# Attention of a hybrid backbone: weights times [values | ones] in full-width products, a PSUM bank per head

## The chip, the cores and the metric

One Trainium2 chip, one of its cores. The metric is the device time of one execution in microseconds, as the median of several runs of the same program.

## The reference

Two layers of a latent-token backbone work on 1024 latent and 256 context tokens of 1024 features. Each layer normalizes and modulates its input, projects it once, and splits the result into three mixers: grouped-query attention (8 heads of 64, 2 heads of keys and values), a long convolution (Hyena), and gated linear attention. Their outputs are normalized per head, put side by side, projected, and added to the stream; a SwiGLU block follows. The part that matters here:

```python
def gqa_attend(q, k, v):
    b, lq = q.shape[:2]
    qg = q.reshape(b, lq, ATTN_KV_HEADS, ATTN_GROUP, HEAD_DIM)
    s = jnp.einsum('bqkgd,bskd->bkgqs', qg, k, preferred_element_type=jnp.float32)
    p = jax.nn.softmax(s, axis=-1).astype(v.dtype)
    o = jnp.einsum('bkgqs,bskd->bqkgd', p, v)
    return o.reshape(b, lq, ATTN_WIDTH)

def head_rms_norm(x, g):
    shp = x.shape
    xh = x.reshape(shp[:-1] + (shp[-1] // HEAD_DIM, HEAD_DIM))
    return rms_norm(xh, g.reshape(-1, HEAD_DIM)).reshape(shp)
```

Latent queries read all 1280 keys, context queries (first layer alone) the 256 context keys. Everything is float32. Since the heads' outputs are RMS-normalized right after, the softmax need not be divided by its sum: with o the undivided output and S the sum of the weights, normalizing o/S with a constant eps is the same as normalizing o with eps times S squared.

## The kernel before, in words

The program is recorded through a tile framework whose scheduler sets the order on each engine; nothing in this part is ordered by hand. `phase1` makes the projections, `phase2` the three mixers, `phase34` the output projection and the SwiGLU. Matmuls of projections, scores and transforms use operands split into a high and a low part (fp32r); a product of two float32 tiles is two passes on TensorE and leaves two records.

In `phase2` the long convolution (`hyena`) is recorded first, then the linear attention (`gla`), then the attention, which the scheduler fills in wherever an engine is free. The eight PSUM banks are dealt to roles (L1380): banks 0 to 2 for the score maxima, 3 and 4 for the scores, bank 5 for the outputs, 6 and 7 for the other two mixers.

The attention runs in jobs: a key-value head, a pair of its query heads, a block of queries (512, 512, and 256 context queries). That is 12 jobs in the first layer and 8 in the second, 20 in all.

- `attn_q` (L1011) prepares a head's queries and finds the row maximum of the scores: for each 128 queries and each block of keys a product into a bank of role 0 and a maximum on VectorE (L1031, L1032), then a transpose brings the maxima to one row of the second operand, Q2. The queries of job i + 1 are recorded ahead of the products of job i.
- `attn_o` (L1040) goes over the key chunks of 128. For each of the two heads: two score products (K1 with Q1, K2 with Q2), then the exponential on ScalarE into a tile p, from a ring of 6 (L1056). Then the product of p with the 64 columns of values: head 0's goes to partitions 0 to 63 of the one output bank, head 1's to partitions 64 to 127, each by one half of the array's columns (L1060). GpSimd adds up the p tiles of each head (L1068).
- `attention` (L1071) then sums the accumulated weights over the partitions by a product with 64 columns of ones per head (L1095), copies the output, squares both, takes the mean square per head by a product with `blk` (L1102), adds eps times the squared sums on VectorE (L1103), and calls `headnorm`, which takes the reciprocal root (`rsqrt`, L189: Ln, Exp and Square on ScalarE, two steps on VectorE) and writes to DRAM.

All three of the outputs, the sums and the mean squares use bank 5 in turn.

```python
            for j in range(2):
                self.mm(X[64 * j:64 * j + 64], V[:, kc], ps[j], kc == k0, kc == 9)
```

## Time and profile before

| | |
|---|---|
| three runs, us | 3710.39 (median), 3722.3, 3709.04 |
| the profiled execution, span | 3712.2 us, 1.8 us above that median; no time of its own outside the span is given |
| PE busy | 3563.2 us, 96% |
| VectorE (DVE) busy | 2014.1 us, 54% |
| GpSimd (POOL) busy | 1353.5 us, 36% |
| ScalarE (ACT) busy | 1088.0 us, 29% |
| mean granted clock of TensorE | 0.978 |

One execution is shown by a hardware profiler. An engine's busy time is the union of its instructions' records. A matmul's record runs on past the point at which the next one starts, so for a stream of matmuls the distance from start to start is its price, and the record's length is not. "PEld" is the load of the stationary operand. L numbers are lines of the kernel.

### The profile page before, as it was taken

The numbers are of one execution on the slowest core, as the hardware profiler recorded it, in microseconds if no ns is written. First come the engines' busy times: TensorE is split into PE (matmuls) and PEld (weight loads), VectorE is DVE, ScalarE is ACT, GpSimd is POOL, SyncE is SP. The second block draws the span as 40 slices with busy tenths as digits, with TensorE's granted clock in tenths as the row PEclk, the third lists the DMA queues.
The fourth block names the chain that finished last, engine by engine and source line by source line (L and its number), as shares of the span: only waits on it lengthen the run. The fifth ranks groups of instructions, "written<-read, shape, count | busy, mean of one in ns | idle before, by whom it ended". The sixth has DMA issues, their size and how long they took to land.

```text
span 3712.2 us, 46254 instructions
## 1 busy us (share of the span) xinstructions
PE 3563.2 (96%) x17903; PEld 2693.5 (73%) x17903; DVE 2014.1 (54%) x3271; ACT 1088.0 (29%) x1956; POOL 1353.5 (36%) x960
## 2 busy tenths in 40 slices
PE   8999899999999999999999899899999999999999
PEld 4789845445677888888888688865445788888887
DVE  6755667863677665644223773757753533223233
ACT  4243233553422111111111333333554421111112
POOL 2424564664333111111111541656764542221221
PEclk9999999999999999999999899999999999999999
DMA  9333311120633323321111333411112421111111
GB/s 329 99 124 123 120 33 43 56 81 20 212 110 99 95 80 89 90 66 54 49 35 46 107 111 116 150 49 42 35 70 71 139 63 51 40 57 46 52 40 57
DMA packets 275804, 310.63 MB, mean 84 GB/s; under 512 B 18680, under 2 KB 205727, under 8 KB 274304
## 3 DMA queue, kind: packets, MB, share of 16 engines
q1 hardware_dynamic: 269279, 287.75, 24.6%
q0 software_dynamic: 2560, 13.89, 1.0%
q10 hardware_dynamic: 3744, 6.03, 0.4%
q8 instruction: 140, 2.29, 0.3%
q14 instruction: 81, 0.66, 0.1%
HBM read 245.75 MB, written 61.87 MB: 83 GB/s over the span
## 4 chain that ended last, share of the span: by engine, by line
PE 75%; DVE 11%; POOL 4%; issue 3%; DMA 3%; ACT 1%; SPq 0%; DVEq 0%; POOLq 0%; ACTq 0%
PE ps L175 74%; PE ps L184 1%; POOL hss L928 1%; DMA nsq<-in_ada_w 1%; POOL hl L187 1%; DVE acc L329 1%; DVE mx L1032 1%; DVE sg L1138 1%; DMA yr<-y_d 0%; DVE h L1537 0%; POOL hy L936 0%; DVE sg L1150 0%; DVE sg L1151 0%; DVE nacc L365 0%; DVE hx L930 0%
## 5 line engine op out<-in xcount | busy, mean ns | idle before, releaser
L175 PE MATMUL ps<-u,hl 128*128 128x512 f32 (+1 forms) x6504 | 1384.4, 372 | 20.6 <-DVE u L403 6.2
L175 PEld LDWEIGHTS ps<-u,hl 128*128 128x128 f32 x6504 | 1136.3, 190 | 252.5 <-issue 14.9
L187 POOL TENSOR_TENSOR hl<-raw,hl 128x1024 fp32r<-128x1024 f32 x148 | 366.5, 2479 | 944.3 <-ACT hl L421 924.5
L175 PE MATMUL ps<-g,w 128*128 128x512 f32 (+1 forms) x2688 | 556.6, 367 | 10.0 <-DVE h L1537 3.4
L175 PEld LDWEIGHTS ps<-g,w 128*128 128x128 f32 x2688 | 466.6, 190 | 95.5 <-DVE h L1537 5.4
L1068 POOL TENSOR_TENSOR ac<-ac,p 128x512 f32<-128x512 f32 x256 | 354.7, 1394 | 159.4 <-ACT p L1057 158.8
L1498 DVE TENSOR_TENSOR s<-ps,s 128x512 f32<-128x512 f32 (+1 forms) x110 | 70.0, 637 | 614.7 <-PE ps L175 597.3
L1537 DVE SCALAR_TENSOR_TENSOR h<-ps,mod,h 128x512 f32<-128x512 f32 (+1 forms) x448 | 303.5, 687 | 181.8 <-PE ps L175 181.6
L175 PE MATMUL ps<-p,V 128*64 128x512 f32 x672 | 309.8, 607 | 4.7 <-ACT p L1057 2.5
L187 POOL TENSOR_TENSOR w<-raw,w 128x1024 fp32r<-128x1024 f32 x44 | 109.0, 2477 | 500.0 <-ACT w L421 499.9
L1032 DVE TENSOR_REDUCE mx<-ps 128x1 f32<-128x512 f32 (+1 forms) x400 | 221.0, 587 | 120.8 <-PE ps L175 119.8
L1057 ACT ACTIVATE p<-ps 128x512 f32<-128x512 f32 (+1 forms) x336 | 194.6, 586 | 286.8 <-PE ps L175 277.7
L175 PEld LDWEIGHTS ps<-Q,K 65*128 65x128 f32 (+1 forms) x672 | 105.0, 191 | 222.2 <-issue 209.8
L421 ACT CAST hl<-raw 128x1024 fp32r<-128x1024 f32 x148 | 154.9, 1049 | 303.9 <-PE ps L175 151.5
L329 DVE SCALAR_TENSOR_TENSOR acc<-nsq,silc,acc 128x512 f32<-128x512 f32 x252 | 210.6, 876 | 61.3 <-DMA nsq<-in_ada_w 60.6
L175 PE MATMUL ps<-Q,K 65*128 65x512 f32 (+1 forms) x672 | 242.2, 442 | 1.2 <-ACT p L1057 1.1
L175 PE MATMUL ps<-y,hl 128*128 128x512 f32 (+1 forms) x960 | 213.8, 381 | 13.2 <-DVE y L187 6.1
L175 PEld LDWEIGHTS ps<-y,hl 128*128 128x128 f32 x960 | 170.8, 194 | 59.3 <-DVE y L187 8.2
L421 ACT CAST w<-raw 128x1024 fp32r<-128x1024 f32 x44 | 46.2, 1051 | 491.8 <-PE ps L175 443.2
L175 PE MATMUL ps<-my,dft 128*128 128x256 f32 (+1 forms) x1176 | 166.8, 294 | 10.3 <-DVE my L187 9.7
L1499 ACT CAST g<-s 128x512 fp32r<-128x512 f32 (+1 forms) x110 | 63.3, 576 | 385.2 <-DVE s L1498 385.2
L175 PEld LDWEIGHTS ps<-my,dft 128*128 128x128 f32 x1176 | 159.1, 203 | 20.6 <-DVE my L187 13.7
(265 smaller groups left out, 4129.2 us busy)
## 6 DMA issues: line engine op xcount, KB each, us to landing
raw<-in_ffn_w SPq DMA_DIRECT2D x132, 512.0 KB
nsq<-in_ada_w SPq DMA_DIRECT2D x144, 256.0 KB
raw<-in_w_in SPq DMA_DIRECT2D x36, 512.0 KB
raw<-in_w_out SPq DMA_DIRECT2D x32, 512.0 KB
ada<-in_ada_w SPq DMA_DIRECT2D x24, 512.0 KB
h_d<-h SPq DMA_DIRECT2D x32, 256.0 KB
dft<-in_c_dft POOLq DMA_DIRECT2D x8, 1024.0 KB, 7.2
qd<-qT_d SPq DMA_DIRECT2D x64, 128.0 KB
```

The source lines that it names most:

```text
L175: self.nc.tensor.matmul(out, w, x, start=start, stop=stop)
L184: self.nc.tensor.transpose(out, in_, self.ident[:n, :n])
L187: eng.tensor_tensor(out=out, in0=x, in1=hi.bitcast(F32), op=ALU.subtract)
L329: nc.vector.scalar_tensor_tensor(out=acc[w], in0=raw, scalar=s, in1=acc[w], op0=ALU.mult, op1=ALU.add)
L421: self.nc.scalar.copy(hi, raw)
L928: nc.gpsimd.tensor_tensor(out=ss, in0=ss, in1=self.mh[:, :nh], op=ALU.pow)
L1032: nc.vector.tensor_reduce(out=mx[:, j, i:i + 1], in_=pm, op=ALU.max, axis=AX.X)
L1057: nc.scalar.activation(p, st, AF.Exp)
L1068: nc.gpsimd.tensor_tensor(out=acc[j], in0=x, in1=ps[j], op=ALU.add)
L1498: nc.vector.tensor_tensor(out=s, in0=p3, in1=s, op=ALU.mult)
L1499: nc.scalar.copy(gs[m][:, 0, o:o + n], s)
L1537: nc.vector.scalar_tensor_tensor(out=h, in0=ps, scalar=self.mod[l][:, 40 + k, w:w + 1], in1=h, op0=ALU.mult, op1=ALU.add)
```

## The change

- The values are stored per key-value head as 192 columns, values, ones, values: `V[:, kvh]`. A memset writes the ones, four loads the values.
- Head 0 takes columns 0 to 127 (values, ones), head 1 columns 64 to 191 (ones, values). A product now fills all 128 columns and one PSUM bank per head: 64 partitions get the outputs, the other 64 get the sum of the weights, once on each partition.
- The additions on GpSimd and the products with ones go.
- ScalarE copies the output halves of both banks into one tile, and squares the sum halves into another, whose halves then lie on the other head's partitions. The mean square and eps times the squared sums come together in one PSUM tile from two products, with `blk` and with `swap` (`blk` with its columns reversed). That tile comes from role 0, the banks of the maxima, and `rsqrt` reads it there.
- Banks: 0 and 1 for the maxima and these mean squares, 2 and 3 for the scores, 4 and 5 for the outputs. The ring of p has 4 tiles.

```diff
+    swap = np.ascontiguousarray(blk[:, ::-1])
...
-                self.V = self.t(ap, [P, 10, P], F32, "V", 1)
-                nc.sync.dma_start(out=self.V, in_=self.v_d)
+                self.V = self.t(ap, [P, 2, 10, 192], F32, "V", 1)
+                nc.gpsimd.memset(self.V[:, :, :, 64:P], 1.0)
+                for kvh in range(2):
+                    for side in (0, P):
+                        nc.sync.dma_start(out=self.V[:, kvh, :, side:side + 64], in_=self.v_d[:, :, 64 * kvh:64 * kvh + 64])
...
-        X = self.ps(2)[:, :n]
+        X = [self.ps(2)[:, :n] for _ in range(2)]
         k0 = 0 if b < 2 else 8
-        acc = [None, None]
...
-                p = self.t(ap, [P, 512], F32, "p", 6)[:, :n]
+                p = self.t(ap, [P, 512], F32, "p", 4)[:, :n]
...
             for j in range(2):
-                self.mm(X[64 * j:64 * j + 64], V[:, kc], ps[j], kc == k0, kc == 9)
-            for j in range(2):
-                if kc == k0:
-                    acc[j] = ps[j]
-                    continue
-                x = acc[j]
-                if kc == k0 + 1:
-                    acc[j] = self.t(ap, [P, 512], F32, "ac", 2)[:, :n]
-                nc.gpsimd.tensor_tensor(out=acc[j], in0=x, in1=ps[j], op=ALU.add)
-        return X, acc
+                self.mm(X[j], V[:, kc, 64 * j:64 * j + P], ps[j], kc == k0, kc == 9)
+        return X
...
-            ps = self.ps(2)[:, :n]
-            for j in range(2):
-                self.mm(ps[64 * j:64 * j + 64], self.ones[:, :64], acc[j], True, True)
             ot = self.t(ap, [P, 512], F32, "ao", 2)[:, :n]
-            nc.scalar.copy(ot, X)
             sq, e = (self.t(ap, [P, 512], F32, "sq", 2)[:, :n] for _ in range(2))
+            for j in range(2):
+                o, t = slice(64 * j, 64 * j + 64), slice(64 - 64 * j, P - 64 * j)
+                nc.scalar.copy(ot[o], X[j][o])
+                nc.scalar.activation(e[t], X[j][t], AF.Square, scale=math.sqrt(EPS))
             nc.scalar.activation(sq, ot, AF.Square)
-            nc.scalar.activation(e, ps, AF.Square, scale=math.sqrt(EPS))
-            v = self.ps(2)[:, :n]
-            self.mm(v, self.blk, sq, True, True)
-            nc.vector.tensor_tensor(out=e, in0=v, in1=e, op=ALU.add)
-            self.headnorm(np_, ot, kvh * 2 + pr, BLK[b][0], n, l, v=e)
+            v = self.ps(0)[:, :n]
+            self.mm(v, self.blk, sq, True, False)
+            self.mm(v, self.swap, e, False, True)
+            self.headnorm(np_, ot, kvh * 2 + pr, BLK[b][0], n, l, v=v)
...
-            self.roles((0, 1, 2), (3, 4), (5,), (6, 7))
+            self.roles((0, 1), (2, 3), (4, 5), (6, 7))
```

The scheduler sets a new order for the whole stretch of the mixers; up to the query projection and from the output projection on, it stays nearly as it was. Three places follow, first the steady part of the first job of the first layer on PE, before. A product `Q,K` is a score, `p,V` weights times values, `K,Q` a product for a maximum; the numbers are the program's tiles.

```order
L175 MATMUL ps_6767<-p_6860,V_4528 64x512
L175 MATMUL ps_6871<-Q_1290_6617,K_830_4538 128x512
L175 MATMUL ps_6871<-Q_1291_6618,K_831_4539 128x512
L175 MATMUL ps_6748<-K_830_4538,Q_1324_6719 128x256
L175 MATMUL ps_6767<-p_6869,V_4528 64x512
L175 MATMUL ps_6880<-Q_1273_6566,K_830_4538 128x512
L175 MATMUL ps_6880<-Q_1274_6567,K_831_4539 128x512
```

The same part of the changed program:

```order
L176 MATMUL ps_6772<-p_6865,V_4528 128x512
L176 MATMUL ps_6874<-Q_1290_6621,K_830_4542 128x512
L176 MATMUL ps_6874<-Q_1291_6622,K_831_4543 128x512
L176 MATMUL ps_6771<-p_6872,V_4528 128x512
L176 MATMUL ps_6881<-Q_1273_6570,K_830_4542 128x512
L176 MATMUL ps_6881<-Q_1274_6571,K_831_4543 128x512
```

The turn of scores and products with values is the same; the products are 128 wide, and go to two output tiles (ps_6771, ps_6772) in place of one. In the first layer 108 products with values stood between the first and the last transform of the convolution before, and 65 stand there now.

Second, PE where the maxima of a latent job stand among the products of the job before it, in the second half of the first layer's attention. Before (`gv,kt` and the product with `shapes` belong to the linear attention):

```order
L175 MATMUL ps_8578<-K_1659_7750,Q_1921_8546 128x512
L175 MATMUL ps_8581<-K_1659_7750,Q_1921_8546 128x512
L175 MATMUL ps_8575<-K_1659_7750,Q_1921_8546 128x256
L184 MATMUL ps_6112<-shapes_64,k_1136_5940 128x128
L175 MATMUL ps_8645<-p_8677,V_4528 64x512
L175 MATMUL ps_8688<-Q_1868_8393,K_1659_7750 128x512
L175 MATMUL ps_8688<-Q_1869_8394,K_1660_7751 128x512
L175 MATMUL ps_6101<-gv_5935,kt_6103 32x64 x4
```

In the changed program, behind the last products of a context job:

```order
L176 MATMUL ps_8369<-p_8390,V_4528 128x256
L176 MATMUL ps_8524<-Q_1869_8320,K_1649_7670 128x512
L176 MATMUL ps_8298<-K_1649_7670,Q_1852_8269 128x256
L176 MATMUL ps_8304<-K_1649_7670,Q_1852_8269 128x512
L176 MATMUL ps_8277<-K_1649_7670,Q_1852_8269 128x512
L176 MATMUL ps_8283<-K_1649_7670,Q_1852_8269 128x512
L176 MATMUL ps_8289<-K_1649_7670,Q_1852_8269 128x256
L176 MATMUL ps_8295<-K_1649_7670,Q_1852_8269 128x512
L176 MATMUL ps_8301<-K_1649_7670,Q_1852_8269 128x512
L176 MATMUL ps_8307<-K_1649_7670,Q_1852_8269 128x256
L176 MATMUL ps_8325<-K_1649_7670,Q_1869_8320 128x512
```

Before, three maxima stood in a row, with three banks for them, and other products followed; now nine stand in a row, with two banks. Over the whole program the runs of three and more are 9, 7, 6, 6, 5, 5, 4 and 3; before they were 5, 4 and 31 of three, with three banks.

Third, POOL beside the convolution of the first layer, before (`t` and `my` are the convolution's, `ac` the sums of weights):

```order
L1234 TENSOR_TENSOR t_917_4982<-t_917_4982,t_918_4983 128x2x128
L1235 TENSOR_TENSOR t_917_4982<-t_917_4982,t_918_4983 128x2x128
L1068 TENSOR_TENSOR ac_6792<-ac_6792,p_6869 128x512
L1068 TENSOR_TENSOR ac_6794<-ac_6794,p_6874 128x512
L187 TENSOR_TENSOR my_4988<-t_917_4982,my_4988 128x512
```

and in the changed program:

```order
L1229 TENSOR_TENSOR t_917_4986<-t_917_4986,t_918_4987 128x2x128
L1230 TENSOR_TENSOR t_917_4986<-t_917_4986,t_918_4987 128x2x128
L188 TENSOR_TENSOR my_4992<-t_917_4986,my_4992 128x512
L1229 TENSOR_TENSOR t_924_5015<-t_924_5015,t_925_5016 128x2x128
L1230 TENSOR_TENSOR t_924_5015<-t_924_5015,t_925_5016 128x2x128
```

The convolution's steps follow one another on POOL with nothing in between.

## Rows read from the trace of the kernel before

**Rows 1.** The page: busy time of each engine, its share of the span, its instructions.

```profile
PE 3563.2 (96%) x17903; PEld 2693.5 (73%) x17903; DVE 2014.1 (54%) x3271; ACT 1088.0 (29%) x1956; POOL 1353.5 (36%) x960
```

**Rows 2.** The page: the chain that ended last, share of the span by engine.

```profile
PE 75%; DVE 11%; POOL 4%; issue 3%; DMA 3%; ACT 1%; SPq 0%; DVEq 0%; POOLq 0%; ACTq 0%
```

**Rows 3.** Busy time of each engine (instructions) in the four stretches; granted clock.

```profile
core 0: us, PE busy (x) PEld busy (x) DVE busy (x) ACT busy (x) POOL busy (x), PEclk, DMA share, GB/s
427.00:787.00 360.00, 336.02 (x1350) 190.07 (x1351) 250.12 (x422) 144.55 (x277) 208.86 (x171) 0.94 0.16 49
787.00:965.00 178.00, 172.60 (x997) 86.00 (x994) 86.78 (x151) 83.99 (x188) 83.16 (x70) 0.99 0.18 61
2410.00:2680.00 270.00, 258.23 (x1072) 147.60 (x1072) 182.59 (x299) 106.98 (x194) 171.06 (x137) 0.98 0.14 44
2680.00:2862.00 182.00, 179.65 (x956) 83.95 (x954) 88.39 (x140) 87.32 (x175) 98.74 (x81) 1.00 0.14 50
sum 990.00, PE 946.49 PEld 507.62 DVE 607.89 ACT 422.83 POOL 561.83; mean PE 236.62 PEld 126.90 DVE 151.97 ACT 105.71 POOL 140.46
```

**Rows 4.** Groups on PE: count | busy us, mean ns | idle before, released by.

```profile
L175 PE MATMUL ps<-p,V 128*64 128x512 f32 x672 | 309.8, 607 | 4.7 <-ACT p L1057 2.5 <-DVE sq L1103 2.1
L175 PE MATMUL ps<-K,Q 128*128 128x512 f32 (+1 forms) x400 | 137.5, 402 | 16.7 <-DVE mx L1032 14.2 <-ACT Q L1037 2.2
L175 PE MATMUL ps<-ac,ones 128*64 128x512 f32 (+1 forms) x80 | 30.5, 586 | 0.0
```

**Rows 5.** Timeline of PE, 669 to 680 us: start, length in us, group.

```profile
669.62 1.02 PE L175 MATMUL ps<-sq,shapes 128*128 128x512 f32 x2
670.08 1.51 PE L175 MATMUL ps<-Q,K 128*128 128x512 f32 x4
671.80 3.65 PE L175 MATMUL ps<-p,V 128*64 128x512 f32 x14 [0.22 <-DVE sq L1103]
675.38 0.74 PE L175 MATMUL ps<-Q,K 128*128 128x512 f32 x2
...
677.05 0.74 PE L175 MATMUL ps<-Q,K 128*128 128x512 f32 x2
677.72 1.07 PE L175 MATMUL ps<-p,V 128*64 128x512 f32 x2
678.72 0.73 PE L175 MATMUL ps<-Q,K 128*128 128x512 f32 x2
679.38 1.07 PE L175 MATMUL ps<-p,V 128*64 128x512 f32 x2
```

**Rows 6.** Timeline of PE: first and last batch, and one of 256 columns.

```profile
529.38 3.65 PE L175 MATMUL ps<-p,V 128*64 128x512 f32 x14 [0.22 <-DVE sq L1103]
...
958.86 1.08 PE L175 MATMUL ps<-p,V 128*64 128x256 f32 x8
...
2848.02 1.08 PE L175 MATMUL ps<-p,V 128*64 128x512 f32 x4
```

**Rows 7.** A stretch of the SwiGLU: busy time by engine (instructions), all matmuls of 512 columns.

```profile
3300.00:3400.00 100.00, 100.00 (x443) 82.81 (x442) 26.37 (x30) 18.40 (x25) 22.99 (x10) 1.00 0.16 48
```

**Rows 8.** Timeline of PE, 2825 to 2827 us.

```profile
2825.16 1.02 PE L175 MATMUL ps<-hn,shapes 128*128 128x512 f32 x2
2826.11 1.07 PE L175 MATMUL ps<-p,V 128*64 128x512 f32 x2
```

**Rows 9.** Groups on POOL: the additions of weights.

```profile
L1068 POOL TENSOR_TENSOR ac<-ac,p 128x512 f32<-128x512 f32 x256 | 354.7, 1394 | 159.4 <-ACT p L1057 158.8
L1068 POOL TENSOR_TENSOR ac<-p,p 128x512 f32<-128x512 f32 (+1 forms) x40 | 49.4, 1238 | 76.4 <-ACT p L1057 41.8 <-PE ps L175 25.0 <-ACT Q L1025 5.7
```

**Rows 10.** Timelines of POOL and DVE, 559 to 576 us.

```profile
559.03 1.28 POOL L1137 TENSOR_TENSOR sg<-sg 128x512 f32<-128x512 f32 x1 [3.83 <-DVE sg L1287]
560.27 3.40 POOL L1068 TENSOR_TENSOR ac<-ac,p 128x512 f32<-128x512 f32 x2
...
559.08 1.38 DVE L1151 TENSOR_TENSOR sg<-sg 128x128 f32<-128x128 f32 x1
...
575.35 0.27 DVE L1151 TENSOR_TENSOR sg<-sg 128x128 f32<-128x128 f32 x1
```

**Rows 11.** Maxima: their group on DVE, and PE's wait, 427 to 787 us.

```profile
L1032 DVE TENSOR_REDUCE mx<-ps 128x1 f32<-128x512 f32 (+1 forms) x400 | 221.0, 587 | 120.8 <-PE ps L175 119.8
...
PE ps L175 <- DVE mx L1032: 7.8, 8, 3.0
```

**Rows 12.** Tile V: loads and first use (count: ns min/median/max, first and last start).

```profile
L175 PEld LDWEIGHTS ps<-p,V x672: 132/136/232, 466.8 to 2848.1; 128*64 128x64 f32 x168
...
L765 SPq DMA_DIRECT2D V<-v_d x2: 328/328/328, 359.7 to 2347.5; - x2
```

**Rows 13.** Groups of the reciprocal root on ACT and DVE.

```profile
L199 ACT ACTIVATE hr<-hr 128x512 f32<-128x512 f32 (+1 forms) x40 | 23.5, 587 | 2.7 <-DVE hyo L991 2.2
L198 ACT ACTIVATE hr<-hr 128x512 f32<-128x512 f32 (+1 forms) x40 | 23.4, 584 | 0.6
...
L200 DVE SCALAR_TENSOR_TENSOR hr<-sq,hr 128x512 f32<-128x512 f32 (+1 forms) x20 | 16.4, 819 | 12.8 <-ACT hr L199 12.8
```

More of the change, by code (lines that the diff above doesn't have):

```diff
@@ L96, in _consts @@
     rot += [np.where(first, 0.5, ca), sa, np.where(first, 0.0, ca), np.where(first, 0.0, ca), np.where(first, 0.5, sa)]
-    c["c_k"] = np.concatenate([np.eye(P, dtype=np.float32), blk, np.stack(rot, 1).astype(np.float32)], 1)
+    c["c_k"] = np.concatenate([np.eye(P, dtype=np.float32), blk, swap, np.stack(rot, 1).astype(np.float32)], 1)
     mind, maxd = math.log(1e-2) / 1.5, math.log(1e-2) / 0.3
@@ L212, in setup @@
         cp = self.const
-        k = self.t(cp, [P, 2 * P + 19], F32, "shapes")
+        k = self.t(cp, [P, 3 * P + 19], F32, "shapes")
         nc.sync.dma_start(out=k, in_=A["c_k"])
-        self.ident, self.blk, self.rot = k[:, 0:P], k[:, P:2 * P], k[:, 2 * P:]
+        self.ident, self.blk, self.swap, self.rot = k[:, 0:P], k[:, P:2 * P], k[:, 2 * P:3 * P], k[:, 3 * P:]
         self.silc = self.t(cp, [P, KC, 2], F32, "silc")
@@ L1008, in attn_kv @@
             self.lo(nc.vector, K1[64:P, x], raw[64:P], K1[64:P, x])
-        return K1, K2, self.V[:, :, 64 * kvh:64 * kvh + 64]
+        return K1, K2, self.V[:, kvh]
     def attn_q(self, ap, h, ops, b):
@@ L1089, in attention @@
             nxt = queries(i + 1)
-            X, acc = self.attn_o(ap, ops[kvh], b, Q)
+            X = self.attn_o(ap, ops[kvh], b, Q)
             Q = nxt
-            ps = self.ps(2)[:, :n]
+            ot = self.t(ap, [P, 512], F32, "ao", 2)[:, :n]
+            sq, e = (self.t(ap, [P, 512], F32, "sq", 2)[:, :n] for _ in range(2))
             for j in range(2):
-                self.mm(ps[64 * j:64 * j + 64], self.ones[:, :64], acc[j], True, True)
-            ot = self.t(ap, [P, 512], F32, "ao", 2)[:, :n]
-            nc.scalar.copy(ot, X)
-            sq, e = (self.t(ap, [P, 512], F32, "sq", 2)[:, :n] for _ in range(2))
+                o, t = slice(64 * j, 64 * j + 64), slice(64 - 64 * j, P - 64 * j)
+                nc.scalar.copy(ot[o], X[j][o])
+                nc.scalar.activation(e[t], X[j][t], AF.Square, scale=math.sqrt(EPS))
             nc.scalar.activation(sq, ot, AF.Square)
-            nc.scalar.activation(e, ps, AF.Square, scale=math.sqrt(EPS))
-            v = self.ps(2)[:, :n]
-            self.mm(v, self.blk, sq, True, True)
-            nc.vector.tensor_tensor(out=e, in0=v, in1=e, op=ALU.add)
-            self.headnorm(np_, ot, kvh * 2 + pr, BLK[b][0], n, l, v=e)
+            v = self.ps(0)[:, :n]
+            self.mm(v, self.blk, sq, True, False)
+            self.mm(v, self.swap, e, False, True)
+            self.headnorm(np_, ot, kvh * 2 + pr, BLK[b][0], n, l, v=v)
     def hyena(self, l, last, hp, np_, dp):
```

## The prediction

> **What bounds the kernel now.** The span is 3712.2 us, 1.8 us above the median of the three runs (3710.39); the sum is made against 3712.2 and 2 us are taken off at the end. Read the engines' shares first: PE is busy 96% of the span, no other engine over 54% [rows 1]. The chain that ended last says the same, 75% PE [rows 2]. A change is therefore worth what it does to PE's time, unless it makes PE wait. The change touches only the mixers, so the stretches come next [rows 3]: attention with the long convolution at 427 to 787 us and 2410 to 2680 us, attention with the linear attention at 787 to 965 and 2680 to 2862. In these 990 us PE is busy 946.5 us, but in the first stretch the clock is granted at 0.94, so some of that is time at 1.2 in place of 2.4 GHz. PE bounds here too; POOL (561.8 us) and DVE (607.9 us) do not, taken as shares.
>
> Then the attention's own groups [rows 4]. A weights-times-values product is float32 and leaves two records, so 672 records are 336 products, 320 of 512 columns and 16 of 256. They go to one half of the array's columns each, head 0 left, head 1 right. What they really cost is not their records' length (607 ns) but the distance to the next start, and for that the timeline is read [rows 5]. From 677.05 to 678.72 one period passes: two score products, then one product with the values. Its start to the next start is 1.00 us (677.72 to 678.72), the two scores take 0.66 (678.72 to 679.38). So the two column halves do **not** overlap there: head 0's product and head 1's stand apart, with scores in between. Where a scheduler put them back to back they do: 14 records, 7 products, in 3.58 us (671.80 to 675.38), 0.51 us each. Counting all of them: 251 stand alone (240 with a score product behind), 85 in 19 batches of two to seven, which take 37 us together; the first and the last batch, and one of 256 columns, are in [rows 6].
>
> **The change part by part.**
> *The lone products.* A float32 product over all 128 columns is already there. It is the sum over 64 features of the squares, sq times a constant: from 669.62 to the end of the four score products behind it (670.08 + 1.51) are 1.97 us; four scores at 0.226 us, the rate of PE where 443 matmuls fill 100 us [rows 7], are 0.90, the last record's tail is about 0.16 (0.40 less 0.24), leaving 0.90 to 0.91; the twin at 2825.16 takes 0.95 with a change of mode behind it [rows 5, 8]. I take 0.87. The scores then run at some 0.46 a pair in place of 0.66, because nothing has to be loaded behind a finished column-half product. A period falls from 1.66 to 1.33, by 0.33 us. For all 250 of 512 columns that is 83 us; if the scores gained nothing it would be 250 times 0.13, 33 us. I take 75, near the upper end, since 240 of 251 have scores behind them.
> *The batches.* 70 products of 512 columns and 15 of 256 now take 37 us; at 0.87 and 0.43 they take 67. That costs 30 us; their own changes of mode (19 times 0.2 us) go, so 27.
> *The sums.* 40 products with ones, 30.5 us of PE [rows 4], go. In their place comes one product with the swap matrix for each of the 20 jobs, at 0.87 or 0.43: 16 us.
> The sums' 30 us may be 25 (records share tails) or 35 (with changes of mode around them). PE therefore gains 75 - 27 + 30 - 16 = **62 us**; from the ends, 33 - 30 + 25 - 16 = 12 to 83 - 25 + 35 - 15 = 78.
>
> *GpSimd.* 296 additions, 404 us, go [rows 9]. POOL is off the path as a share, but it slows DVE: the same fold of 128 x 128 takes DVE 0.27 us at 575.35 and 1.38 us at 559.08, while POOL adds at 559.03 and 560.27 [rows 10]. Of the chain 11% is DVE [rows 2], which would be 69 us of the 630 us of the two convolution stretches, an estimate; if a seventh of that is waiting of this kind, 10 us come back. None and 30 us are the bounds. I take 10.
> *PSUM.* The maxima's banks fall from three to two, the values' rise from one to two, the scores keep two. A maximum takes DVE 0.59 us [rows 11], its product PE 0.23, so with two banks each product behind the second of a run waits about 0.4 us. The order now has runs of 9, 7, 6, 6, 5, 5, 4 and 3 maxima without other work, 29 behind the second; before, with three banks, nearly every run was three or less. 29 times 0.4 is 12 us lost. Where DVE is held up by convolution work it is more (the waits of PE for maxima are 7.8 us in the first stretch already [rows 11]); bounds 5 and 40.
> *Fewer fillers.* The new order puts 65 products with values beside the first layer's convolution in place of 108. Nothing in the trace shows how long the convolution is without cover: between no loss and 30 us. I take 5 lost: DVE is freer by then.
> *At nothing.* ScalarE: five evictions a job in place of three, about 1.1 us by 20 jobs, on an engine busy 29%. DVE loses one addition a job. Four loads of V in place of one, and a memset: V is asked for at 359.7 us and first used at 466.8 [rows 12]; if that cover went, a few us. Weight buffers 6 to 4 a ring: exp (0.59 us) ends before the 1.33 us till its product, so the ring need not be longer.
> Sum: 62 + 10 - 12 - 5 = 55; 3712 - 55 - 2 = **3655 us**. All good ends together, 78 + 30 - 5 - 0, would be 103 us and 3607; all bad ones, 12 + 0 - 40 - 30, 58 us the other way and 3768.
>
> **The rule that speaks against it.** In [rows 5] the halves overlap in a batch, at 0.51 us a product, and not elsewhere. The Trainium skill, TensorEngine Tiling (Array Packing), sections Overview and Performance Considerations, offers up to twice the speed for outputs of 64 columns; by that the full width would be a loss. What the sum would be by it is worked out as rival 4, from the batches' rate.
>
> **The rivals.**
> 1. *Relief.* POOL's additions were what stretched the convolution; with them gone the first stretches shorten by more, and the half-clock spells with them. For: the clock of 0.94 and 24 us of idle PE in 427 to 787 [rows 3]. Against: only 11% of the chain is DVE [rows 2]. 40 us more: about 3610.
> 2. *Given back.* The convolution's own chain, now with less beside it, becomes the bound; PE's 62 us turn into idle time. For: 43 fewer products beside it, and POOL, ACT and DVE take turns in it. Against: PE was 93% busy there. About 3705, no change.
> 3. *Slower: the banks of the maxima.* The mean square of job i now takes a maxima bank and keeps it until Ln, Exp, Square (0.58 us each) and a DVE step of 0.82 are done, 2.6 us at the least [rows 13]; job i + 2's maxima stand behind it, PE in order behind them. It decides from a wait of 3.7 us a job (55 + 19 over 20 jobs); with exps and convolution steps ahead on ACT and DVE it could be 5 us a job, 100 us: 3755. Against: PE waited for maxima only 14.2 us in all before [rows 4], and the order has other products behind most of them.
> 4. *The halves overlap more than starts show.* If a lone product really cost 0.51 us, with what follows running in the other half, full width would add 0.36 by 250, 90 us, and 30 for the batches, less 14 for the sums: about 3815. Against: the next product starts 1.00 us later, period by period [rows 5].
>
> **How the numbers follow.** A measurement of this kernel can tell about 0.5%, 18.6 us, from no change: faster is below 3691.8, slower above 3729. Chances: the forecast 0.60 (its own range 3625 to 3690), rival 1 0.13, rival 2 0.17, rival 3 0.07, rival 4 0.03. Faster: 0.60 + 0.13 + 0.03 of rival 2 = 0.76. Same: 0.13 of rival 2 and 0.02 of rival 3 = 0.15. Slower: 0.01 + 0.05 + 0.03 = 0.09. The range of 3605 to 3700 leaves out most of rivals 3 and 4, the upper half of rival 2 and the far end of rival 1.
>
> **What would show it.** Right: in the timeline of the changed kernel, a period of two scores and one product with values of about 1.33 us, at any place in either layer; 336 full-width products at 0.87 us; POOL's time in the four stretches down by 404 us; DVE's folds near their short times. The stretches together (990 us before) some 55 us shorter, the rest of the program within a few us. Wrong: a period still near 1.66, or one of 1.33 while PE's idle time in the stretches grows by more than 40 us, with the maxima (rival 3) or the convolution's steps (rival 2) as what ended it; or a granted clock well below 0.94 there.

## The result, and the profile after

The changed kernel takes 3739.6 us (median of 10 runs, 3729.3 to 3744.8) against 3715.2 us (10 runs, 3709.0 to 3727.5) for the kernel before on the same chip: a ratio of **1.0055, 95% interval 1.0042 to 1.0069**. It is slower by 24 us where 55 us of gain were forecast, and outside the range.

The page of the changed kernel, busy time of each engine (span 3737.3 us), beside [rows 1]; then span and mean granted clock:

```profile
PE 3542.7 (95%) x17863; PEld 2795.7 (75%) x17863; DVE 1940.0 (52%) x3251; ACT 1110.5 (30%) x1996; POOL 944.7 (25%) x666
```

```profile
core 0: 3737.3 us, clock 0.966
```

The same line of the kernel before:

```profile
core 0: 3712.2 us, clock 0.978
```

POOL has lost its 409 us as it should (1353.5 to 944.7). PE is busy 20.5 us less, yet the span is 25.1 us longer, so PE's idle time went from 149.0 to 194.6 us. And PE worked longer at its lower clock: the span times (1 - clock) is 127 us after, 82 before. (This takes all half-clock time as lost, some of which PE was idle in, and the clock has three digits: good to some 2 us.) Taking both off the span leaves PE's work at full clock: **3481.5 us before, 3415.6 after, 66 us less.** The forecast had 62 for it. So the gain on PE is there, and 46 us of idle time and 45 us of slow clock ate it. The question is where those 91 us come from.

First the gain itself. The timeline of PE in the changed kernel, 876 to 881 us, where no wait falls in the attention (start, length, group, as in [rows 5]):

```profile
876.71 1.02 PE L176 MATMUL ps<-p,V 128*128 128x512 f32 x2
877.17 1.03 PE L176 MATMUL ps<-Q,K 128*128 128x512 f32 x2
878.03 1.02 PE L176 MATMUL ps<-p,V 128*128 128x512 f32 x2
878.49 1.03 PE L176 MATMUL ps<-Q,K 128*128 128x512 f32 x2
879.36 1.02 PE L176 MATMUL ps<-p,V 128*128 128x512 f32 x2
```

876.71, 878.03, 879.36: the period is 1.32 to 1.33 us, as forecast, in place of 1.66. Within it the shares are the other way round (0.46 behind the product with values, 0.86 behind the scores). Starts give the length of a period, not whose it is.

Then the stages. In the changed kernel the convolution ends at 691 us (781 before), the linear attention runs from there to 850, and attention's tail with the output projection follows to 1129, where SwiGLU begins (1102 before). Layer 1 has the same three stages. Busy time by stage, columns as in [rows 3]:

```profile
423.00:691.00 268.00, 225.07 (x1053) 163.54 (x1052) 182.35 (x335) 105.65 (x204) 77.50 (x79) 0.92 0.21 67
691.00:850.00 159.00, 154.86 (x909) 98.85 (x907) 73.21 (x143) 71.07 (x160) 12.68 (x15) 0.86 0.20 69
850.00:1129.00 279.00, 248.41 (x987) 170.17 (x986) 150.26 (x232) 108.19 (x189) 46.32 (x23) 0.93 0.34 104
2425.00:2618.00 193.00, 169.45 (x813) 126.52 (x814) 128.27 (x227) 70.56 (x129) 63.16 (x66) 0.92 0.20 65
2618.00:2785.00 167.00, 161.78 (x916) 97.05 (x916) 89.28 (x160) 84.97 (x173) 16.12 (x16) 0.98 0.20 68
2785.00:2978.00 193.00, 180.43 (x670) 122.89 (x669) 87.66 (x126) 89.37 (x143) 50.12 (x33) 0.99 0.28 88
```

Layer 0 carries the loss: it ends 27 us later (1129 in place of 1102), and the second layer adds nothing to that. PE idles 43 us in the first stage and 31 us in the third, and in the second it is 97% busy at a granted clock of only 0.86. What PE waits for (us, times, longest), and the maxima's products with the wait ahead of them, beside [rows 4, 11]:

```profile
PE ps L176 <- DVE mx L1037: 32.0, 44, 2.8
```

```profile
L176 PE MATMUL ps<-K,Q 128*128 128x512 f32 (+1 forms) x400 | 158.9, 429 | 35.0 <-DVE mx L1037 25.7 <-ACT Q L1042 5.8 <-DVE hr L201 3.0
```

14.2 us before, 32.0 now: maxima are the largest single cause, though only 18 of the 46 us. How they wait is in the timelines of PE from 889 to 898 us and of DVE from 895 us:

```profile
889.16 0.28 PE L176 MATMUL ps<-K,Q 128*128 128x256 f32 x1
889.96 0.50 PE L176 MATMUL ps<-K,Q 128*128 128x512 f32 x1 [0.52 <-DVE mx L1037]
891.84 0.49 PE L176 MATMUL ps<-K,Q 128*128 128x512 f32 x1 [1.38 <-DVE hr L201]
893.17 0.50 PE L176 MATMUL ps<-K,Q 128*128 128x512 f32 x1 [0.83 <-DVE mx L1037]
894.46 0.58 PE L176 MATMUL ps<-K,Q 128*128 128x256 f32 x1 [0.78 <-DVE mx L1037]
895.56 0.80 PE L176 MATMUL ps<-K,Q 128*128 128x512 f32 x1 [0.52 <-DVE mx L1037]
897.14 0.79 PE L176 MATMUL ps<-K,Q 128*128 128x512 f32 x1 [0.78 <-DVE mx L1037]
```

```profile
895.08 0.42 DVE L1037 TENSOR_REDUCE mx<-ps 128x1 f32<-128x256 f32 x1 [0.68 <-PE ps L176]
896.39 0.69 DVE L1037 TENSOR_REDUCE mx<-ps 128x1 f32<-128x512 f32 x1 [0.89 <-PE ps L176]
897.97 0.69 DVE L1037 TENSOR_REDUCE mx<-ps 128x1 f32<-128x512 f32 x1 [0.88 <-PE ps L176]
```

PE waits for DVE and DVE for PE, in turn: product, maximum, product, maximum, 1.1 to 1.6 us a round. Two banks should let one engine work while the other does. The order of PE's instructions says why they don't. Here its PSUM tiles are named by bank (B0 and B1 are the maxima's, role 0) and the rest of each name is cut. Rows of other products are left out; the numbers jump there:

```
1727 MATMUL B0 <- K1, Q1 128x512 [waits DVE]
1731 MATMUL B1 <- sq, shapes 128x512 [waits Activation]
1732 MATMUL B1 <- sq, shapes 128x512
1733 MATMUL B0 <- K1, Q1 128x512 [waits DVE]
1738 MATMUL B0 <- K1, Q1 128x256 [waits DVE]
1739 MATMUL B0 <- K1, Q1 128x512 [waits DVE]
1740 MATMUL B1 <- K1, Q1 128x512 [waits DVE]
1741 MATMUL B1 <- K1, Q1 128x512 [waits DVE]
1742 MATMUL B1 <- K1, Q1 128x256 [waits DVE]
1743 MATMUL B1 <- K1, Q1 128x512 [waits DVE]
```

Row 1731 is a job's mean square (885.88 us in the trace); it holds B1 until the reciprocal root's last reading (L201) ends, which is what releases row 1740 at 891.84. The maxima of a later job's first head that have their turn on B0 go through first, each behind the one before; then those of B1, alone again. Little else is ready: the next latent job's products need these maxima. The six maxima from 611 to 624 us stand on B1 alone in the same way; there DVE has steps of the convolution in between, so that a round takes up to 3.5 us.

The mean square is not the only holder. In PE's order over the whole program, 99 of the 400 products for maxima go to the same bank as the one ahead of them; in the kernel before, with three banks, 9. Of the 14 rows of three or more on one bank, six have a mean square on the other bank, and eight the tile of the transposes, which is of role 0 too: it takes its turn in the ring, and it cannot be filled before all 12 maxima of its head are done.

At such places and near them the granted clock is low. Windows of the changed kernel, and one of the kernel before for the linear attention's small products (columns as above):

```profile
605.00:645.00 40.00, 23.33 (x77) 13.75 (x77) 36.86 (x66) 17.05 (x35) 7.71 (x7) 0.74 0.21 66
730.00:747.00 17.00, 15.14 (x117) 8.49 (x117) 11.66 (x27) 8.65 (x29) 0.00 (x0) 0.60 0.06 22
747.00:754.00 7.00, 7.00 (x48) 5.10 (x46) 4.33 (x8) 0.35 (x1) 0.00 (x0) 0.98 0.00 0
754.00:785.00 31.00, 31.00 (x177) 22.04 (x176) 5.64 (x10) 5.51 (x11) 2.53 (x2) 0.51 0.07 18
888.00:914.00 26.00, 17.47 (x39) 9.51 (x39) 14.58 (x26) 4.31 (x10) 0.00 (x0) 0.67 0.05 16
```

```profile
865.00:895.00 30.00, 30.00 (x211) 17.11 (x211) 8.02 (x15) 8.49 (x17) 11.40 (x9) 1.00 0.06 11
```

### The profile page after: what moved, and what is told of

It is laid out like the page before. It is cut to its first block, busy times and chain, and to the rows that moved or that the text cites. A ratio compares the mean times of both kernels' runs of the same rounds, so it can differ in the third digit from the quotient of the medians.

```text
span 3737.3 us, 45624 instructions
## 1 busy us (share of the span) xinstructions
PE 3542.7 (95%) x17863; PEld 2795.7 (75%) x17863; DVE 1940.0 (52%) x3251; ACT 1110.5 (30%) x1996; POOL 944.7 (25%) x666
## 5 line engine op out<-in xcount | busy, mean ns | idle before, releaser
L176 PE MATMUL ps<-p,V 128*128 128x512 f32 x672 | 345.0, 596 | 7.2 <-ACT p L1061 7.0
L176 PE MATMUL ps<-Q,K 65*128 65x512 f32 (+1 forms) x672 | 339.6, 582 | 0.8 <-ACT Q L1042 0.8
L1037 DVE TENSOR_REDUCE mx<-ps 128x1 f32<-128x512 f32 (+1 forms) x400 | 229.5, 590 | 193.1 <-PE ps L176 191.8
L176 PEld LDWEIGHTS ps<-Q,K 65*128 65x128 f32 (+1 forms) x672 | 128.8, 192 | 149.1 <-issue 146.1
L176 PE MATMUL ps<-K,Q 128*128 128x512 f32 (+1 forms) x400 | 158.9, 429 | 35.0 <-DVE mx L1037 25.7
```

What stands on the lines that cost most here:

```text
L176: self.nc.tensor.matmul(out, w, x, start=start, stop=stop)
L1037: nc.vector.tensor_reduce(out=mx[:, j, i:i + 1], in_=pm, op=ALU.max, axis=AX.X)
```

## The experiments

Three theories at the start: **A**, the mean square holds a maxima bank; **B**, two banks are too few for the maxima, whoever holds them; **C**, attention loses its cover because the convolution ends earlier. All times are medians against fresh runs of the kernel before; the last three columns are worked out from span, PE's busy time and clock of the one profiled execution, as above (for e13 that execution is 14 us above the median, for e5 8 us below). The last column is no fixed property of a kernel: before, e3, e4, e7, e9, e10, e13 and e14 issue the same PE instructions, and in their different orders it runs from 3462 to 3502 us.

| kernel | us | ratio to before, 95% interval | PE idle | lost to the clock | PE's work at full clock |
|---|---|---|---|---|---|
| before | 3715 to 3720 | | 149 | 82 | 3482 |
| after | 3739.6 | 1.0055, 1.0042 to 1.0069 | 195 | 127 | 3416 |
| e1_v_values | 3706.5 | 0.9962, 0.9949 to 0.9975 | 193 | 100 | 3410 |
| e2_v_sbuf | 3720.2 | 1.0003, 0.9991 to 1.0015 | 181 | 130 | 3407 |
| e3_before_two | 3814.9 | 1.0252, 1.0234 to 1.0269 | 191 | 126 | 3494 |
| e4_before_ring4 | 3723.5 | 1.0011, 0.9999 to 1.0022 | 145 | 78 | 3493 |
| e5_heads_three | 3630.6 | 0.9757, 0.9739 to 0.9775 | 138 | 80 | 3403 |
| e6_heads_two | 3694.9 | 0.9938, 0.9924 to 0.9952 | 169 | 107 | 3416 |
| e7_before_nosums | 3691.1 | 0.9920, 0.9906 to 0.9934 | 141 | 89 | 3462 |
| e8_heads_three_v2 | 3618.8 | 0.9725, 0.9707 to 0.9743 | 139 | 76 | 3402 |
| e9_before_turn | 3761.3 | 1.0126, 1.0106 to 1.0147 | 160 | 109 | 3493 |
| e10_before_turn_nosums | 3698.3 | 0.9955, 0.9939 to 0.9971 | 129 | 89 | 3477 |
| e11_order | 3622.5 | 0.9751, 0.9730 to 0.9772 | 138 | 83 | 3399 |
| e12_one_score | 3779.3 | 1.0169, 1.0148 to 1.0190 | 221 | 113 | 3438 |
| e13_two_together | 3819.6 | 1.0274, 1.0258 to 1.0291 | 188 | 142 | 3502 |
| e14_two_turn | 3738.6 | 1.0062, 1.0048 to 1.0077 | 159 | 78 | 3498 |

### The held bank and the number of banks: e1 to e4

e1, in the changed kernel:

```diff
-            v = self.ps(0)[:, :n]
+            v = self.ps(2)[:, :n]
```

> The changed kernel, with the mean square of a job put into the values' two banks in place of the maxima's two. Three theories of what ate the 53 us that the attention's own products gained (changed kernel: 3739.6 us; PE idle +32 us and +58 us of work at half clock in layer 0). A, the held bank: the mean square holds one of the two maxima banks until its reciprocal root is done, the next job's maxima go through the other one alone; then PE's waits for maxima fall from 32 us to about 15, the spells at half clock shrink with them, and the time is about 3700. B, two banks: two banks are too few for the maxima, whoever holds them; then waits and time stay, 3730 to 3745. C, lost cover: without GpSimd's additions the convolution ends earlier (691 us in place of 781) and attention is left alone behind it; the time stays, 3730 to 3745, and the convolution still ends near 690.

3706.5 us, 33 us under the changed kernel. So the held bank costs something, against B and C; but PE's waits for maxima fell to 19.9 only, and its idle time hardly at all, since the new order has another wait, for the output projection's additions:

```profile
PE ps L176 <- DVE h L1560: 33.5, 4, 16.2
PE ps L176 <- DVE mx L1037: 19.9, 33, 2.2
```

What e1 gained is clock, 100 us lost in place of 127. A is a part of the cause and not the whole.

e2, in the changed kernel:

```diff
             self.mm(v, self.swap, e, False, True)
-            self.headnorm(np_, ot, kvh * 2 + pr, BLK[b][0], n, l, v=v)
+            nc.scalar.copy(e, v)
+            self.headnorm(np_, ot, kvh * 2 + pr, BLK[b][0], n, l, v=e)
```

> The changed kernel, with the mean square copied by ScalarE from its maxima bank to the tile of the squared sums at once, and the reciprocal root taken from the copy: the bank is held some 0.6 us after its products in place of 2.6 us and more. A, the held bank: most of what e1 gives, 3700 to 3715. B, two banks, and C, lost cover: no change, 3730 to 3745; 20 copies of 0.6 us on ScalarE are no cost.

3720.2 us, 19 us gained, less than A had. The bank is held for less time, and still held; but PE's waits for maxima are 33.3 us, no shorter than in the changed kernel, so where the 19 us come from is not shown.

e3, in the kernel before:

```diff
-            self.roles((0, 1, 2), (3, 4), (5,), (6, 7))
+            self.roles((0, 1), (3, 4), (5,), (6, 7))
```

> The kernel before with two banks for the maxima, 0 and 1, in place of three (bank 2 lies idle), all else as it was: 64-column products, GpSimd's sums, mean square in the values' bank. A, the held bank: nothing holds a maxima bank, so within 8 us of before (3715). B, two banks: PE's waits for maxima go from 14 us to some 30, with spells at half clock behind them: 3735 to 3760. C, lost cover: within 8 us of before, the convolution ends near 781 us.

95 us slower, far above what any theory had. No mean square is in these banks, so B holds and A alone does not. The rows on a single bank are there all the same: 83 of the 400 products for maxima follow one on their own bank, and in all 17 rows of three or more it is the tile of the transposes that comes next on the other bank. The waits for maxima are only 11 us more than before; the rest of the loss is in the table: 42 us of idle time in all (21 of it the wait for the output projection's additions that e1 has too) and 44 us of clock.

```profile
PE ps L175 <- DVE mx L1032: 25.6, 34, 3.1
```

e4, in the kernel before:

```diff
-                p = self.t(ap, [P, 512], F32, "p", 6)[:, :n]
+                p = self.t(ap, [P, 512], F32, "p", 4)[:, :n]
```

> The kernel before with a ring of four weight tiles in place of six, all else as it was (GpSimd's additions read the weights too, so a tile comes free later here than in the changed kernel). A, B and C: within 10 us of before (3715). A fourth theory, D, the short ring: exp has to wait for a tile, PE for exp; 3730 or more, and PE's waits for the weights above the 3.6 us of before.

3723.5 us, within the noise. D falls; the ring was rightly costed at nothing.

### The third bank given back: e5, e6, e8, e12

With a bank per head there are no three banks for the maxima, unless one head is done after the other. e5, in the changed kernel (the evictions of a head follow its last product):

```diff
-        X = [self.ps(2)[:, :n] for _ in range(2)]
...
-        for kc in range(k0, 10):
...
-            for j in range(2):
...
+        for j in range(2):
...
+            X = self.ps(2)[:, :n]
+            for kc in range(k0, 10):
...
-                self.mm(X[j], V[:, kc, 64 * j:64 * j + P], ps[j], kc == k0, kc == 9)
+                self.mm(X, V[:, kc, 64 * j:64 * j + P], p, kc == k0, kc == 9)
+            yield X
...
-            self.roles((0, 1), (2, 3), (4, 5), (6, 7))
+            self.roles((0, 1, 2), (3, 4), (5,), (6, 7))
```

> The changed kernel with its two heads one after the other in a job, each over all keys: one bank holds the values of one head, and bank 2 goes back to the maxima, which have three as before. The mean square stays in a maxima bank. e3 took one bank from the maxima of the kernel before and cost 95 us, e1 took the mean square out of them and gave 33 us. Theory B now (two banks for three are the main loss): the loss goes, the gain of the products (53 us by starts, 62 forecast) comes out, 3650 to 3685. Theory A (the held bank alone): the mean square is still there, though with three banks it leaves two; 3695 to 3720. Theory C (attention without cover behind the convolution, whatever the banks): 3725 to 3745.

e6, in e5:

```diff
-            self.roles((0, 1, 2), (3, 4), (5,), (6, 7))
+            self.roles((0, 1), (3, 4), (5,), (6, 7))
```

> As e5, heads one after the other with one bank for the values, but two banks for the maxima (0 and 1; bank 2 lies idle). It tells the order of the heads from the number of banks. Theory B: as the changed kernel, 3725 to 3760, so that e5 less e6 is the price of the third bank, 60 us or more. If heads in turn are what helps: as e5.

3630.6 and 3694.9 us. The third bank is worth 64 us, by an edit of the roles alone (the scheduler's order is new, as in every pair here). e5 is below even what B forecast, and far from A and C. C is done for: the convolution of e5 ends at 697 us, as early as in the changed kernel, and nothing is lost. e6 is 45 us better than the changed kernel, which B had not expected.

e8, in e5, is e1 and e2 together:

```diff
-            v = self.ps(0)[:, :n]
+            v = self.ps(2)[:, :n]
...
+            nc.scalar.copy(e, v)
-            self.headnorm(np_, ot, kvh * 2 + pr, BLK[b][0], n, l, v=v)
+            self.headnorm(np_, ot, kvh * 2 + pr, BLK[b][0], n, l, v=e)
```

> As e5 (heads one after the other, three maxima banks), and the mean square in the values' bank, copied at once by ScalarE to the tile of the squared sums, so that nothing but maxima and the turn of the maxima uses their banks. Theories A and B: the best of all, 3640 to 3675, 10 to 30 us under e5 if the held bank still costs something with three banks. Theory C: 3725 or more. Against it: the next job's first product with values waits for the copy, some 2 us a job without other work, 40 us at most.

3618.8 us, 101 us under the kernel before and the fastest of all that compute the whole. Against e5 the gain is 12 us and the intervals touch, so with three banks the held bank is worth little. Nor are rows on a single bank the price by themselves: in e5, with the mean square in the ring of three, 65 products for maxima still follow one on their own bank, in e8 5. PE's waits for maxima in e5, in e6 and in e8:

```profile
PE ps L176 <- DVE mx L1037: 11.8, 15, 3.5
```

```profile
PE ps L176 <- DVE mx L1037: 24.4, 33, 2.0
```

```profile
PE ps L176 <- DVE mx L1037: 5.6, 10, 0.8
```

e12, in the changed kernel:

```diff
-            self.roles((0, 1), (2, 3), (4, 5), (6, 7))
+            self.roles((0, 1, 2), (3,), (4, 5), (6, 7))
```

> The changed kernel as it is, heads together with two banks for the values and the mean square in a maxima bank, but three banks for the maxima and one for the scores in place of two and two. Theory B: the third maxima bank gives back 60 us or so, the single score bank costs some of it (a score has to wait for exp, 0.59 us, 16 us for each key chunk of a pair at the worst without other work): 3690 to 3735. If maxima banks are not what hurts: well above 3740.

3779.3 us, well above 3740, which by the words of the expectation speaks against B. But PE's longest wait is now for exp, so the single score bank costs something that was not there before, and the run cannot tell the two apart; the waits for maxima are 25.3 us in place of 32.0. (The "16 us" in that text has no source; a score's wait for exp is some 0.6 us.)

```profile
PE ps L176 <- ACT p L1061: 49.3, 80, 1.4
```

### GpSimd's additions, and the turn of the heads: e7, e9, e10, e13, e14

e7, in the kernel before:

```diff
-            for j in range(2):
-                if kc == k0:
-                    acc[j] = ps[j]
-                    continue
...
-                nc.gpsimd.tensor_tensor(out=acc[j], in0=x, in1=ps[j], op=ALU.add)
+            acc = ps
```

> The kernel before without GpSimd's 296 additions: the products with ones take the last pair of weight tiles alone, so the sums, and with them the output, are not the reference's. Products of 64 columns and three maxima banks as before. The forecast had 10 us for GpSimd's additions (none to 30): 3685 to 3715. Theory C: the convolution ends some 90 us earlier than 781 us, near 690, and attention left alone behind it makes PE wait or fall to half clock: 3715 to 3745.

3691.1 us: with three maxima banks the additions cost 29 us, at the top of the forecast's bounds. The convolution's end moves from 781 to 736 us and the time falls, against C. DVE is busy 1923.9 us in place of 2014.1 [rows 1]; its folds beside POOL [rows 10] are the plainest. Kernel before, then e7:

```profile
L1151 DVE TENSOR_TENSOR sg<-sg 128x128 f32<-128x128 f32 x12 | 7.7, 643 | 0.0
```

```profile
L1144 DVE TENSOR_TENSOR sg<-sg 128x128 f32<-128x128 f32 x12 | 4.0, 329 | 0.0
```

e9, in the kernel before, with the additions inside the same loop; e10 is e9 with `acc[j] = p` in place of the additions:

```diff
-        for kc in range(k0, 10):
-            ps = []
-            for j in range(2):
-                Q1, Q2 = Q[j]
+        for j in range(2):
+            Q1, Q2 = Q[j]
+            for kc in range(k0, 10):
...
-                self.mm(X[64 * j:64 * j + 64], V[:, kc], ps[j], kc == k0, kc == 9)
+                self.mm(X[64 * j:64 * j + 64], V[:, kc], p, kc == k0, kc == 9)
```

> The kernel before with the two heads of a job one after the other, each over all keys, all else as it was (products of 64 columns, GpSimd's sums, three maxima banks, one bank for both heads' values). From the changed kernel to e6 the turn of the heads gave 45 us with two maxima banks. Theory E1, the turn helps because a job can start when 12 maxima of one head are done in place of 24 of two, whatever the banks: 3665 to 3700. Theory E2, it only repairs the shortage of banks: 3705 to 3725.

> As e9, without GpSimd's additions (the products with ones take the last weight tile of each head alone, so the output is not the reference's). It leaves one thing between it and e5: the width of the product with the values and what comes with it. If the turn and the additions add up: e9 less 29 us (what e7 gave). The width's own price, e5 (3630.6) less this kernel: by the starts (p,V, scores, sums and swap products) -40 to -55 us, by the forecast -62; if the halves of the array overlapped more than the starts show (rival 4), e5 would be the slower one.

e9 is slower by 46 us, which neither E1 nor E2 had; with the additions gone (e10) the turn costs 7 us against e7, so what costs in e9 comes with GpSimd's sums. How was not looked into further. The use of e10 is that it differs from e5 by the width and what comes with it (swap products in place of those with ones, the mean square in a maxima bank, evictions by halves, the ring of 4): 3698.3 to 3630.6 is **68 us for the full width**, idle time and clock together being the same in both (218 us in the table).

e13 and e14 are e7 and e10 with two maxima banks, by the edit of e3.

> The kernel before without GpSimd's additions (as e7: the products with ones take the last weight tiles, the output is not the reference's), heads together, with two maxima banks in place of three. With full width the third bank could be priced only with the heads in turn (64 us). E2, the turn of the heads repairs part of the shortage: here, together, the bank is worth the 64 us and the 45 us that the turn gave, about 110: 3785 to 3815. E1, the turn helps by itself, whatever the banks (it did not with three: e10 against e7, +7 us): 3745 to 3765.

> As e13 with the heads one after the other (as e10, two maxima banks). E2: 40 us or more below e13, and some 64 us above e10 (3698): 3745 to 3775. E1: the same distance from e13 as e10 has from e7, so within 10 us of e13.

Now the four corners, all with 64 columns and no additions:

| us | three banks | two banks | the bank's price |
|---|---|---|---|
| heads together | 3691.1 (e7) | 3819.6 (e13) | 128 |
| heads in turn | 3698.3 (e10) | 3738.6 (e14) | 40 |

E2 holds: the turn is worth nothing with three banks (7 us the other way) and 81 us with two, and the third bank is worth most, 128 us, with the heads together, as the changed kernel has them; E2 had 110 there, and 64 where e14 shows 40. But the two-bank price is not all wait for maxima. PE's longest wait in e14, and its wait for maxima:

```profile
PE ps L175 <- DVE h L1555: 30.9, 4, 17.3
PE ps L175 <- DVE mx L1032: 6.1, 12, 0.8
```

In e10 the first of these is not among the waits at all, and the second is 3.9 us. So e14, which idles 29 us more than e10 in all, waits 31 us more at the output projection, behind the attention, and only 2 us more at the maxima. This wait comes and goes with the order: none in the kernel before, 5.6 us in the changed one, 33.5 in e1, 22.2 in e7, 31.1 in e13. An edit of the banks sets all of the order anew, and the prices here are those of bank and order together.

The prices do not simply add up, either. The additions are worth 29 us with three banks (before, e7) and nothing with two (e3 3814.9, e13 3819.6); the width is worth 68 us in e10 and e5, 44 in e14 and e6, and 80 in e13 and the changed kernel. One way from the kernel before to the changed one, a pair of kernels for each step, is: -29 (additions, e7), +7 (turn, e10), -68 (width, e5), +64 (the bank, e6), +45 (heads together again, changed kernel), from 3720 to 3739.

e11, in e8:

```diff
-        jobs = [(kvh, pr, b) for kvh in range(2) for pr in range(2) for b in ([0, 1] if last else [0, 1, 2])]
+        jobs = [(kvh, pr, b) for kvh in range(2) for bs in ([[0, 1]] if last else [[0, 1], [2]]) for pr in range(2) for b in bs]
```

> As e8, and in layer 0 the short jobs (context queries, two key chunks) of a key head stand together behind its four long ones, so that a long job's 24 maxima stand behind a short job twice in place of four times. If what is left of the wait for maxima sits behind short jobs: 5 to 15 us under e8 (3618.8). If e8 has none left (PE's waits for maxima are no longer among its longest): within 8 us.

3622.5 us, no difference from e8, and PE's waits for maxima are 7.4 us in place of 5.6: what is left of them does not sit behind short jobs.

## Why the prediction was wrong

*The lone products, the batches, the sums on PE* (forecast 62 us gained): **right** in mechanism and sign. The period went from 1.66 to 1.33 us as said, though with the shares the other way round. The size is 66 us by the page and 68 by e10 and e5, but 44 and 80 by the other two pairs, so that it comes within a few us of 62 is in part luck. e5 against e10 gains, where by rival 4 full width had to lose: the halves stood together only in batches [rows 5, 6]. The Trainium skill (TensorEngine Tiling (Array Packing), section Overview) gives a speedup of up to two for outputs of 64 columns; the lone products here, 1.00 us from start to start, had none of it, and those in a batch, 0.51 us, had.

*GpSimd* (10 us, none to 30): right in sign, **under-sized**; 29 us. The forecast took a seventh of DVE's share of the chain [rows 2]; DVE's busy time alone fell by 90 us. It also misread its example: what POOL does from 559.03 us, beside the slow fold, is a fold of the convolution itself (L1137 in [rows 10]), which stays; the addition begins at 560.27, when that fold is nearly over. And with two maxima banks, as the changed kernel has them, e3 and e13 show no gain from the additions.

**PSUM (12 us lost, 5 to 40): this step failed.** A bank less for the maxima measures 95 us in the kernel before (e3), 128 without the additions (e7, e13), and 40 to 64 with the heads in turn (e10 and e14, e5 and e6); in the changed kernel it is the 109 us from e5 to it, the turn among them. The step took each maximum behind the second of a run to cost 0.4 us, 29 times. Three things were wrong with it. Two banks were taken to be two banks: but the scheduler hands maxima to the banks in turn in the program's order, and where one bank is held, by a mean square or by the transposes' tile, it sends those that have the other bank ahead, so that products and maxima alternate on a single bank, 1.1 to 1.6 us a round where a maximum alone is 0.59 [rows 11]. By PE's waits for maxima this is 18 us. The order was at hand before the run and shows it once the banks are named. Second, a run of maxima was counted as its own waits; but the next job's scores wait behind it, and with the heads together they need all 24 maxima of both. That is the program's order; what it costs was not measured apart. The heads in turn win 45 to 81 us with two banks and nothing with three; that it is the 12 maxima in place of 24 which does it is argued, not shown. Third, no term of the sum had the clock: 45 us of the loss is time at 1.2 in place of 2.4 GHz, about 30 of them in layer 0's three stages, and [rows 3] had shown 0.94 in a stretch with idle PE already.

*Rival 3* named the right banks and the right holder, the mean square, at 0.07. As it was worked out, it is the smaller part: 33 us with two banks (e1). That its 3755 lies near the 3739.6 measured is luck. The forecast held that other products stand behind most maxima ([rows 4], 14.2 us of wait in all); that was the order of three banks.

*Fewer fillers* (5 us): not found; C fell in e5 and e7. *Rival 2*, the convolution as the bound, has the right symptom, idle PE, mostly by the wrong hand: PE's waits for the convolution's steps (`my`) grew by 8 us, those for maxima by 18. *At nothing*: the ring, 3.5 us and within the noise (e4); evictions, loads of V and the memset were not tried one by one, and e5 and e8 contain them.

Of the signs named, "a granted clock well below 0.94" came true (0.86 in the second stage). Idle time up by more than 40 us, with the maxima as the largest releaser, came true over the program (46 us); the stretches meant, convolution and linear attention in both layers, have 32 us of it, and most of the rest lies in the attention's tails behind them.

That a bank held up sets the rows of maxima on a single bank is read from order and timeline; that the number of banks is the cause is shown by e3, e6, e13 and e14, each of which differs from its pair in the roles of the banks and in nothing else of the program. In e3 the other holder, the transposes' tile, is read from the order. How the bank turns into time is not shown in full: the waits for maxima grow by 2 to 18 us only, and the rest is clock, PE's work in another order, and waits elsewhere.

## What to carry to other kernels

A bank taken from a ring that two engines share is not costed by its count. Name the banks in the instruction order and look who holds each for how long; a ring of two with one long holder is a ring of one for as long as it is held. The tile that holds a bank need not be new: the transposes' tile was in the ring of three before. The Trainium skill (Perfetto Trace Analysis, section Matmuls) has the rule that matmul groups should go through different banks so that the reading of one overlaps the next; here it was worth 40 to 128 us for one bank, against 68 us that the change gained by taking it.

When several heads or tiles start on the same precondition, try one after the other: the first needs half of it. It gave 45 to 81 us where banks were short; where they were plenty it cost 7 us, and 46 with GpSimd's additions still there (e9).

## What the runs showed of the hardware

The granted clock fell in a stretch in which the trace shows PE without a gap (the profile models the ends of matmuls, so that a short one could be hidden). From 747 to 754 us PE is busy 7.00 of 7 us at 0.98, and from 754 to 785 us 31.00 of 31 us at 0.51 (the windows above): in the latter almost only the linear attention's products, of 32 rows or 64 columns, with a few maxima and norms between. One group of eight in the changed kernel, and the same group of the kernel before, which ran among weights-times-values products and scores at 1.00 (window 865 to 895):

```profile
772.56 1.12 PE L176 MATMUL ps<-A,gv 128*64 128x128 f32 x8
```

```profile
869.26 0.66 PE L175 MATMUL ps<-A,gv 128*64 128x128 f32 x8
```

The Trainium skill (TensorE: Matmul & The Clock Gate, section A second HAM failure mode: psum-queue depth-cycling) puts a falling clock down to small idle times of PE between groups of matmuls as banks are cycled; the windows at 605 and 888 us, with PE 58% and 67% busy at 0.74 and 0.67, agree, and this one, without idle time, does not. The large products that stood among the small ones before are missing in it, since the scores wait for their maxima; that this brought the clock down is not shown, as no run changed it alone.
